# A transformer block's down projection in a seven-product form: 14 of 16 row pairs by seven block products instead of eight, two of the four weight sums made by adding transfers, and rows scaled by their norm before they are transposed

## The chip, the cores and the metric

One Trainium2 chip, one core of it. The time is the device time of one execution in microseconds. Three timed executions of the kernel before gave 305.18, 305.67 and 305.17 us (median 305.18); another execution was taken by the profiler and took 305.3 us, of which the span from the first to the last instruction is 303.2 us. TensorE (PE) multiplies matrices, VectorE (DVE) and ScalarE (ACT) work element by element, GpSimd (POOL) does a little of both kinds of odd work, and SyncE (SP) issues most transfers (DMAs).

## What is computed

One block on 256 rows of width 1024, all in float32: an attention mixer, a residual, and a squared-ReLU MLP with 4096 hidden columns, each between two RMS norms.

```python
h = x
u = rms_norm(h, norm_mix_pre)
u = moba_attention(u, w_qkv, w_o)          # 8 heads of 128; 256 rows are one block, so: causal, with slopes
h = h + rms_norm(u, norm_mix_post)
u = rms_norm(h, norm_ffn_pre)
u = square(relu(u @ w_up)) @ w_down        # w_up 1024 x 4096, w_down 4096 x 1024
h = h + rms_norm(u, norm_ffn_post)
```

## The kernel before

**Three matmuls for one product.** Every float32 operand is split into a high part (a copy rounded to the matmul's float32r type) and a low part (the rest). A product is three matmuls into one accumulator: high by high, high by low, low by high (`mm3`, lines 209 to 214). So each weight element passes ScalarE once (`whi`, line 83) and VectorE once (`wlo`, line 84), before TensorE can use it.

**The weights' pipeline.** The class `Weights` holds a list of 48 sources of 1 MB each: attention's, then the MLP's. `load` issues a source's transfer on SP into one of five raw buffers; `pump` splits the next quarter of a source (512 elements per partition: one instruction on ScalarE, one on VectorE) into one of four pairs of part buffers, and issues the next load when all four quarters of a source are split. `done` frees part buffers. The MLP's sources come as chunks of 512 hidden columns: `up0, up1, down0, up2, down1` and so on, `down7` last.

**The order of the work.** PE and SP run in the order in which the code is written. ScalarE and VectorE do so too in the stretches under `manual_schedule`; elsewhere a scheduler sets their order. PE runs through attention, then the out projection `o0`, `o1` (tiles `acc`), and then the MLP. The 256 rows are two tiles `t` of 128.

**From attention to the MLP** (lines 589 to 646). `PostNorm.take` squares and weighs a finished half row out of PSUM, `put` adds the residual into `xs`. The rows of tile 0 are transposed on PE (tile `ht`) from `xs`, in the middle of `o1`'s last 12 matmuls; `evac_x` takes them out of PSUM times the gain, as a high and a low part (`xT`). The transposed rows are not yet divided by their norm: this factor, `rstd2` (from `square_x` and `rstd_of`, whose power is taken on POOL), is applied later. For chunk 0, which has rows as PSUM's partitions (`up_first`, 512-column matmuls), it is a scalar per partition in the ReLU; for the other chunks, which have hidden columns as partitions, it is a row `rrow2` that `diag_of` and `row_of` make with four VectorE instructions and two matmuls.

**The MLP's loop** (lines 648 to 676). `up_chunk(c)`: 4 hidden blocks by 8 by 3 = 96 matmuls of 256 columns, and for each hidden block `up_evac` (ReLU and norm on VectorE, two squares on ScalarE, a difference on VectorE). `down_chunk(c - 1)`: 4 hidden blocks by 2 row tiles by 2 column halves by 3 = 48 matmuls of 512 columns into four accumulators `acd` that stay in PSUM to the end. Seen as pairs of hidden blocks, there are 16 pairs, and each pair takes 8 block products, 24 matmuls. The last chunk's down projection runs row tile by row tile (lines 682 to 690), with the last norm, the residual and the output's transfers behind each.

Of the kernel before, what the change touches and what calls it, by code (L numbers as in the profile page):

```python
# [8 lines left out]
F32 = mybir.dt.float32  # L9
# [12 lines left out]


# [4 lines left out]
class Weights:  # L28
# [4 lines left out]
    N = 2048  # L33

    def __init__(self, nc, raw_pool, part_pool, raw_bufs, part_bufs):
        self.nc, self.raw_pool, self.part_pool = nc, raw_pool, part_pool
        self.raw_bufs, self.part_bufs = raw_bufs, part_bufs
        self.sources, self.raw, self.parts, self.steps, self.split = [], {}, {}, [], set()
        self.loaded = self.finished = self.next = self.part = 0

    def add(self, src, how, cuts=1):
        self.sources.append((src, how, cuts))
        return len(self.sources) - 1

    def load(self, n=None):
# [17 lines left out]
    def slice(self, t, i, j):  # L63
        how = self.sources[i][1]
        if how == "cols":
            return t[:, :, j * P:(j + 1) * P]
        if how == "rows":
            return t[:, j // 2, (j % 2) * 512:(j % 2) * 512 + 512]
        return t[:, j, :]

    def pump(self, n, lo_engine=None):
        nc = self.nc
        while n > 0 and self.next < len(self.steps):
            i, j = self.steps[self.next]
            if i >= self.finished + self.part_bufs or i >= self.loaded:
                return
            if i not in self.parts:
                shape = list(self.raw[i].shape)
                self.parts[i] = [self.part_pool.tile(shape, F32R, name=f"w{p}{i}", tag=f"w{p}", bufs=self.part_bufs)
                                 for p in ("hi", "lo")]  # L80
            hi, lo = (self.slice(t, i, j) for t in self.parts[i])
            x = self.slice(self.raw[i], i, j)
            nc.scalar.activation(hi, x, AF.Copy)  # L83
            (lo_engine or nc.vector).tensor_tensor(lo, x, f32(hi), op=ALU.subtract)  # L84
            self.split.add((i, j))
            self.next += 1
            n -= 1
            if sum((i, q) in self.split for q in range(4)) == 4:
                self.load()

    def get(self, i, j):
        while (i, j) not in self.split:
# [3 lines left out]
        return self.parts[i]  # L96
# [6 lines left out]
def block(ctx: ExitStack, tc: tile.TileContext, x, g_mix_pre, g_mix_post, g_ffn_pre, g_ffn_post,  # L103
# [80 lines left out]

    ident = const.tile([P, P], F32, name="ident")
# [8 lines left out]
    dist = const.tile([P, 384], F32, name="dist")  # L194
# [12 lines left out]
    oT = [const.tile([P, HEADS, S], F32R, name=f"oT{i}") for i in range(2)]  # L207

    def mm3(ps, a, b, start, stop):


        nc.tensor.matmul(ps, lhsT=a[0], rhs=b[0], start=start, stop=False)  # L212
        nc.tensor.matmul(ps, lhsT=a[0], rhs=b[1], start=False, stop=False)  # L213
        nc.tensor.matmul(ps, lhsT=a[1], rhs=b[0], start=False, stop=stop)  # L214
# [38 lines left out]
    def transpose_x(k, t):  # L253
        o = (k // 4) * S + t * P
        nc.tensor.transpose(banks[k % 4][:, o:o + P], xs[:, t, k * P:(k + 1) * P], ident)

    def evac_x(k, g0, a=0, b=S):
        o = (k // 4) * S
        split_psum_scaled((xT[0][:, k, a:b], xT[1][:, k, a:b]), banks[k % 4][:, o + a:o + b],
                          gT[:, g0 + k:g0 + k + 1])  # L260
# [10 lines left out]

    qk_pool = tc.alloc_tile_pool(name="qk_pool", bufs=1)
# [443 lines left out]
```

## Time and profile before

| | |
|---|---|
| timed executions | 305.17, 305.18, 305.67 us |
| profiled execution, its span | 305.3 us, 303.2 us |
| granted TensorE clock, mean | 0.997 |
| PE busy | 294.5 us, 97% |
| weight loads on PE | 262.7 us, 87% |
| DVE busy | 194.5 us, 64% |
| ACT busy | 166.6 us, 55% |
| POOL busy | 18.5 us, 6% |
| read from HBM | 52.44 MB, 176 GB/s over the span |

A row of the timeline has the start, the duration, the engine, the line, the operation, and output<-inputs with their shapes; `[idle before <-releaser]` says how long the engine stood idle and what ended that. Rows of PE overlap: a matmul's row is longer than the step to the next one, and the step is what counts. In the groups by line, `x28 | 11.9, 424` is 28 instructions, 11.9 us in all, 424 ns each.

### The profile page before, as it was taken

Reading aid. Unit: us, or ns where it says so; the run is one execution under the profiler, and the core shown is the slowest. Engines: PE = TensorE matmul, PEld = TensorE weight load, DVE = VectorE, ACT = ScalarE, POOL = GpSimd, SP = SyncE. Lnnn points to the kernel's source line nnn. Section 1 sums busy time; section 2 is a strip of 40 time slices with the busy share of each in tenths; the row PEclk is TensorE's granted clock in tenths of the full one; section 3 lists DMA queues with packets and bytes.
Section 4 is the critical chain, followed back from the end, with each engine's and each line's share of the span. In section 5 each row is a group of like instructions: output and inputs, shape, how many; then the busy total and the mean of one; then the engine's idle time right before and its main releaser. Section 6 shows DMA issues by size and latency. Waiting matters only on the chain.

```text
span 303.2 us, 4863 instructions
## 1 busy us (share of the span) xinstructions
PE 294.5 (97%) x1838; PEld 262.7 (87%) x1838; DVE 194.5 (64%) x407; ACT 166.6 (55%) x395; POOL 18.5 (6%) x34
## 2 busy tenths in 40 slices
PE   7999999999999999999999999999999999999991
PEld 3889999988998888898898898898898898898880
DVE  2668989774689395999447547547547537537042
ACT  4767938665396265977526526526526526526020
POOL 4000133101200001000000000000000000000000
PEclk9999999999999999999999999999999999999998
DMA  6998595729404740087960960960950950300012
GB/s 189 367 394 308 200 391 176 268 99 378 148 2 145 272 118 22 0 291 262 332 228 9 344 205 11 334 211 11 347 197 16 338 203 10 130 0 3 0 45 93
DMA packets 22055, 53.79 MB, mean 177 GB/s; under 512 B 1024, under 2 KB 1808, under 8 KB 22032
## 3 DMA queue, kind: packets, MB, share of 16 engines
q1 hardware_dynamic: 21888, 53.16, 50.5%
q8 instruction: 14, 0.23, 0.3%
q10 hardware_dynamic: 144, 0.33, 0.3%
q14 instruction: 9, 0.07, 0.1%
HBM read 52.44 MB, written 1.05 MB: 176 GB/s over the span
## 4 chain that ended last, share of the span: by engine, by line
PE 93%; DVE 4%; DMA 1%; ACT 0%; issue 0%; DVEq 0%; ACTq 0%
PE psu L212 10%; PE psu L214 10%; PE psu L213 10%; PE acd L212 10%; PE acd L213 10%; PE acd L214 10%; PE psv L292 3%; PE psq L212 3%; PE psq L213 3%; PE psq L214 3%; PE psv L294 2%; PE acc L214 2%; PE acc L212 2%; PE psv L296 2%; PE acc L213 2%; DVE wlo L84 2%
## 5 line engine op out<-in xcount | busy, mean ns | idle before, releaser
L84 DVE TENSOR_TENSOR wlo<-raw,whi 128x512 fp32r<-128x512 f32 x186 | 121.0, 699 | 42.3 <-ACT whi L83 42.1
L83 ACT ACTIVATE whi<-raw 128x512 fp32r<-128x512 f32 x192 | 107.2, 623 | 47.6 <-PE acd L214 33.3
L212 PE MATMUL psu<-xT,whi 128*128 128x256 f32 x224 | 63.4, 283 | 0.0
L213 PE MATMUL psu<-xT,whi 128*128 128x256 f32 x224 | 63.3, 282 | 0.0
L214 PE MATMUL psu<-xT,wlo 128*128 128x256 f32 x224 | 62.9, 281 | 0.0
L213 PE MATMUL acd<-wlo,uhi 128*128 128x512 f32 x128 | 50.5, 395 | 0.0
L212 PE MATMUL acd<-whi,uhi 128*128 128x512 f32 x128 | 50.5, 395 | 0.0
L214 PE MATMUL acd<-whi,ulo 128*128 128x512 f32 x128 | 50.5, 394 | 0.0
L214 PEld LDWEIGHTS psu<-xT,wlo 128*128 128x128 f32 x224 | 42.5, 190 | 0.0
L213 PEld LDWEIGHTS psu<-xT,whi 128*128 128x128 f32 x224 | 42.1, 188 | 0.3
L212 PEld LDWEIGHTS psu<-xT,whi 128*128 128x128 f32 x224 | 42.0, 187 | 0.3
L556 ACT ACTIVATE uhi<-r 128x256 fp32r<-128x256 f32 x28 | 11.6, 413 | 35.0 <-DVE r L555 35.0
L214 PEld LDWEIGHTS acd<-whi,ulo 128*128 128x128 f32 x128 | 24.1, 188 | 5.6
L213 PEld LDWEIGHTS acd<-wlo,uhi 128*128 128x128 f32 x128 | 24.1, 188 | 5.3
L212 PEld LDWEIGHTS acd<-whi,uhi 128*128 128x128 f32 x128 | 24.1, 188 | 5.3
L558 DVE TENSOR_TENSOR ulo<-u,uhi 128x256 fp32r<-128x256 f32 x28 | 11.9, 424 | 14.4 <-ACT u L557 14.4
L555 DVE SCALAR_TENSOR_TENSOR r<-psu,rrow 128x256 f32<-128x256 f32 x28 | 11.8, 422 | 13.7 <-PE psu L214 13.7
L212 PE MATMUL psq<-xT,whi 128*128 128x256 f32 x64 | 18.4, 288 | 0.0
L212 PE MATMUL psk<-xT,whi 128*128 128x256 f32 x64 | 18.4, 287 | 0.0
L214 PE MATMUL psq<-xT,wlo 128*128 128x256 f32 x64 | 18.1, 282 | 0.0
L213 PE MATMUL psq<-xT,whi 128*128 128x256 f32 x64 | 18.1, 282 | 0.0
L214 PE MATMUL psk<-xT,wlo 128*128 128x256 f32 x64 | 18.0, 282 | 0.0
(121 smaller groups left out, 432.7 us busy)
## 6 DMA issues: line engine op xcount, KB each, us to landing
raw<-in_w_up_dram SPq DMA_DIRECT2D x16, 1024.0 KB, 6.1
raw<-in_w_down_dram SPq DMA_DIRECT2D x16, 1024.0 KB, 7.5
raw<-in_attn_w_qkv_dram SPq DMA_DIRECT2D x10, 1024.0 KB, 8.6
raw<-in_attn_w_o_dram SPq DMA_DIRECT2D x4, 1024.0 KB, 4.9
raw<-in_attn_w_qkv_dram SPq DMA_DIRECT2D x8, 256.0 KB, 6.2
xs<-in_x_dram SPq DMA_DIRECT2D x2, 256.0 KB, 6.0
xs<-in_x_dram SPq DMA_DIRECT2D x1, 512.0 KB, 7.1
g_mix<-in_norm_mix_post_dram SPq DMA_DIRECT2D x1, 512.0 KB, 7.2
```

The source lines that it names most:

```text
L83: nc.scalar.activation(hi, x, AF.Copy)
L84: (lo_engine or nc.vector).tensor_tensor(lo, x, f32(hi), op=ALU.subtract)
L212: nc.tensor.matmul(ps, lhsT=a[0], rhs=b[0], start=start, stop=False)
L213: nc.tensor.matmul(ps, lhsT=a[0], rhs=b[1], start=False, stop=False)
L214: nc.tensor.matmul(ps, lhsT=a[1], rhs=b[0], start=False, stop=stop)
L292: nc.tensor.matmul(psv[0][t], lhsT=x0[t], rhs=w[0], start=first, stop=False)
L294: nc.tensor.matmul(psv[0][t], lhsT=x1[t], rhs=w[0], start=False, stop=False)
L296: nc.tensor.matmul(psv[0][t], lhsT=x0[t], rhs=w[1], start=False, stop=last)
L555: nc.vector.scalar_tensor_tensor(r, ps[:, :S], 0.0, rrow2, op0=ALU.max, op1=ALU.mult)
L556: nc.scalar.activation(hi, r, AF.Square)
L558: nc.vector.tensor_tensor(lo, u, f32(hi), op=ALU.subtract)
```

## The change

**Seven products for a pair.** For a pair `q` of hidden blocks (two blocks of 128 hidden columns), the hidden values form a 2 by 2 grid of blocks (two row tiles, two hidden blocks), and so does the down weight (two hidden blocks, two column halves of 512). The seven-product form (Winograd's variant of Strassen's) replaces the 8 block products by 7, on 4 sums of hidden blocks and 4 sums of weight blocks. The sums of the results are linear, so each of the seven products accumulates over 14 pairs in a PSUM bank of its own (`M1` to `M7`), and they are combined once, after pair 13. Pairs 14 and 15 are added in the plain form onto the combined accumulators.

**Where the sums are made.** Hidden sums: three VectorE instructions per pair (`combine`). Weight sums: two of the four are made by transfers: SP loads one block of the weights twice side by side (`sums`, tag `sum`), and later POOL issues a transfer that adds two other blocks onto them (`accum_op=add`). The other two sums are two VectorE additions (`add_up`). A pair's down weights are now two units of split work: `blocks` (3 blocks, 1536 elements per partition) and `sums` (4 blocks, 2048).

**Larger split instructions, a fixed order.** In the MLP a whole unit is split by one instruction on ScalarE (`W.hi`) and one on VectorE (`W.lo`); ScalarE, VectorE and POOL follow the written order to the end. The up projection goes pair by pair (`up_pair`, 48 matmuls of 256 columns, with 1 KB per partition row of its load), one PSUM bank for both hidden blocks; the down projection of pair `q - 2` follows it.

**Rows divided by their norm first.** `scale_h` takes `rstd2` and writes the scaled rows into `yg` before they are transposed, so that `rrow2`, `diag_of` and `row_of` go for the MLP. The hidden values then need only a ReLU and a square, both on ScalarE.

The core of the diff:

```diff
+    def load(self, n=None):
...
+        if i in self.sevens:
+            self.raw[i] = self.raw_pool.tile([P, 3, 512], F32, name=f"raw{i}", tag="raw", bufs=self.raw_bufs)
+            self.nc.sync.dma_start(self.raw[i][:, 0:1, :], src[:, 0:1, 0:512])
+            self.nc.sync.dma_start(self.raw[i][:, 1:3, :], src[:, 1, :].rearrange("p (h c) -> p h c", c=512))
...
+    def sum_by_loads(self):
+        nc = self.nc
+        for i in self.to_add:
...
+            nc.gpsimd.dma_start(self.sums[i][:, 0:2, :], both, accum_op=ALU.add)
+        self.to_add = []
+        while self.begun < min(len(self.sevens), self.summed + self.SUM_BUFS):
...
+            nc.sync.dma_start(self.sums[i][:, 0:2, :], self.sources[i][0][:, 0:1, 512:1024].broadcast_to([P, 2, 512]))
+            self.to_add.append(i)
+    def add_up(self, u):
...
+        self.nc.vector.tensor_tensor(t[:, 2, :], raw[:, 2, :], t[:, 0, :], op=ALU.add)
+        self.nc.vector.tensor_tensor(t[:, 3, :], raw[:, 1, :], t[:, 2, :], op=ALU.add)
+    def hi(self, u, h=None):
...
+        self.nc.scalar.activation(self.half(self.parts[u][0], h), self.half(x, h), AF.Copy)
+    def lo(self, u, h=None):
...
+        self.nc.vector.tensor_tensor(lo, x, f32(hi), op=ALU.subtract)
...
+        if kind == "sums":
+            self.summed += 1
+            self.sum_by_loads()
+        else:
+            self.load()
...
+    PRODUCTS = (("M1", A11, 0, 0), ("M2", A12, 0, 1), ("M3", S4, 0, 2), ("M5", S1, 1, 0),
+                ("M7", S3, 1, 1), ("M6", S2, 1, 2), ("M4", A22, 1, 3))
...
+    def combine(q):
+        x = hidden[q]
+        tt = nc.vector.tensor_tensor
+        tt(x[:, S3:S1 + 1, :], x[:, A11:A22 + 1, :], x[:, A21:A21 + 1, :].broadcast_to([P, 2, P]), op=ALU.subtract)
+        tt(x[:, S2, :], x[:, S1, :], x[:, A11, :], op=ALU.add)
+        tt(x[:, S4, :], x[:, A12, :], x[:, S2, :], op=ALU.subtract)
...
+        def scale_h(t):
+            rstd_of(ssq2[:, 0, t:t + 1], ssq2[:, 1, t:t + 1], rstd2[:, t:t + 1])
+            for c in range(2):
+                s = slice(c * 512, (c + 1) * 512)
+                nc.vector.tensor_scalar(yg[:, t, s], xs[:, t, s], rstd2[:, t:t + 1], None, op0=ALU.mult)
...
         for c in range(2):
             norms[0].put(xs, c * 512, (c + 1) * 512)
+            square_x(0, ssq2, (c,))
+        scale_h(0)
         last_rows("o1", act_o, 1, 0)
         norms[1].take(0)
-        last_rows("o1", act_o, 1, 1, turn_first)
+        last_rows("o1", act_o, 1, 1)
...
+        W.sum_by_loads()
+        for k in range(KT):
+            transpose_x(k, 0, yg)
+        evac_x(0, KT, 0, P)
+        evac_x(1, KT, 0, P)
         norms[1].take(1)
+        for k in range(2, 5):
+            evac_x(k, KT, 0, P)
...
+        scale_h(1)
+        W.sum_by_loads()
...
         for k in range(KT):
             up_first(0, k)
-            if k == 4:
-                turn(0, 1, 2, 3)
+        for k in range(KT):
+            transpose_x(k, 1, yg)
...
+    def down_pair(q, products):
+        hi, lo = act[q]
+        for name, slot, e, j in products:
...
+            mm3(M[name], a, w, q == 0, q == NP - 3)
+        W.done(1)
...
+        for q in range(4, NP):
+            d = q - LAG
+            if q + 1 < NP:
+                W.hi(piece[f"up{q + 1}"])
+                combine(q - 1)
+            hidden_hi(q - 1)
+            if q + 1 < NP:
+                W.lo(piece[f"up{q + 1}"])
+            hidden_lo(q - 1)
+            below = piece[f"down{d + 1}"]
+            if d + 2 < NP - 1:
+                W.add_up(below + 1)
+            ps = up_pair(q)
...
+            up_relu(q, ps)
+            if q + 1 < NP:
+                W.hi(below)
+            W.lo(below)
...
+            down_pair(d, PRODUCTS[:3])
+            W.hi(below + 1)
+            up_square(q)
+            W.lo(below + 1)
+            down_pair(d, PRODUCTS[3:])
...
+        nc.scalar.activation(m1, M["M1"], AF.Copy)
+        tt(u2, m1, M["M6"], op=ALU.subtract)
+        tt(M["M2"], M["M2"], m1, op=ALU.add)
+        tt(u3, M["M7"], u2, op=ALU.add)
+        tt(u4, M["M5"], u2, op=ALU.add)
+        nc.vector.scalar_tensor_tensor(M["M5"], M["M5"], -1.0, u3, op0=ALU.mult, op1=ALU.subtract)
+        tt(M["M4"], M["M4"], u3, op=ALU.add)
+        tt(M["M3"], M["M3"], u4, op=ALU.subtract)
```

**What moves on PE.** At the end of `o1`, before: the eight transposes of tile 0 (`ht`) stand between the last 12 matmuls of `acc` (row 682 comes after the same four tiles a second time).

```order
673 L214 MATMUL acc_1_1195<-whi_1208,oT_124 128x512
674 L255 MATMUL ht_1354<-ident,xs 128x128
675 L255 MATMUL ht_1355<-ident,xs 128x128
676 L255 MATMUL ht_1356<-ident,xs 128x128
677 L255 MATMUL ht_1357<-ident,xs 128x128
682 L212 MATMUL acc_1_1195<-whi_1208,oT_123 128x512
```

In the changed kernel they stand behind all of `acc`, directly ahead of the first matmul of `up_first` (`psu_0`), and read the scaled rows `yg` (again the four tiles come twice).

```order
682 L301 MATMUL acc_1_1198<-whi_1299,oT_130 128x512
683 L343 MATMUL ht_1356<-ident,yg 128x128
684 L343 MATMUL ht_1357<-ident,yg 128x128
685 L343 MATMUL ht_1358<-ident,yg 128x128
686 L343 MATMUL ht_1359<-ident,yg 128x128
691 L299 MATMUL psu_0_1522<-whi_1366,xT_127 128x512
```

The same is done with tile 1: its transposes stood inside `up_first`, and now stand between `up_first(0, ...)` and `up_first(1, ...)`.

**What moves on VectorE there.** Before, at the same place: the residual of tile 0 (`xs`), the first half of tile 1's norm (`mss`, `yg`), and at once the low parts of the transposed rows.

```order
168 L533 SCALAR_TENSOR_TENSOR xs<-yg,rs,xs 128x512 x2
169 L527 TENSOR_SCALAR mss<-ss 128x1
170 L530 TENSOR_TENSOR yg<-acc_0_1194,g_mix 128x512
171 L222 SCALAR_TENSOR_TENSOR xT_122<-ht_1354,gT,xT_121 128x128
172 L222 SCALAR_TENSOR_TENSOR xT_122<-ht_1355,gT,xT_121 128x128
```

In the changed kernel the mean square (`ms`) and the scaling (`yg<-xs,rstd`) come in between, and the second half of tile 1's norm stands between the low parts.

```order
168 L623 SCALAR_TENSOR_TENSOR xs<-yg,rs,xs 128x512 x2
169 L318 SCALAR_TENSOR_TENSOR ms<-ssq_1352 128x1
170 L719 TENSOR_SCALAR yg<-xs,rstd_1353 128x512 x2
171 L617 TENSOR_SCALAR mss<-ss 128x1
172 L620 TENSOR_TENSOR yg<-acc_0_1197,g_mix 128x512
173 L352 SCALAR_TENSOR_TENSOR xT_128<-ht_1356,gT,xT_127 128x128
174 L352 SCALAR_TENSOR_TENSOR xT_128<-ht_1357,gT,xT_127 128x128
175 L617 TENSOR_SCALAR mss<-ss,mss 128x1
```

**VectorE in the MLP's loop.** In the changed kernel one pair's work reads as follows: the hidden sums (`x`), the low parts of the next up weights and of the hidden blocks (`ulo`), the two weight sums, and the low parts of the pair's `blocks` and `sums`.

```order
249 L655 TENSOR_TENSOR x_2150<-x_2150 128x256
250 L656 TENSOR_TENSOR x_2150<-x_2150 128x128
251 L657 TENSOR_TENSOR x_2150<-x_2150 128x128
252 L134 TENSOR_TENSOR wlo_2169<-raw_1972,whi_2168 128x2048
253 L671 TENSOR_TENSOR ulo_2175<-x_2150,uhi_2174 128x896
254 L114 TENSOR_TENSOR sum_1948<-raw_2032,sum_1948 128x512
255 L115 TENSOR_TENSOR sum_1948<-raw_2032,sum_1948 128x512
256 L134 TENSOR_TENSOR wlo_2235<-raw_2032,whi_2234 128x1536
257 L134 TENSOR_TENSOR wlo_2251<-sum_1948,whi_2250 128x2048
```

Before, a pair had eight quarters `wlo` of 512 elements (two units) and two rows each of `r` and `ulo` (256 elements). All that stands ahead of `o1`'s norms is in the same order in both kernels on PE, VectorE and ScalarE.

More of the change, by code (lines that the diff above doesn't have):

```diff
@@ L28 @@
 class Weights:
-    N = 2048
+    STEPS = {"cols": 4, "k": 4, "rows": 4, "whole": 1, "blocks": 1, "sums": 1}
+    SUM_BUFS = 3
     def __init__(self, nc, raw_pool, part_pool, raw_bufs, part_bufs):
@@ new lines, in add_up, with half @@
+    def add_up(self, u):
+        i, _ = self.units[u]
+        raw, t = self.raw[i], self.sums[i]
+        self.nc.vector.tensor_tensor(t[:, 2, :], raw[:, 2, :], t[:, 0, :], op=ALU.add)
+        self.nc.vector.tensor_tensor(t[:, 3, :], raw[:, 1, :], t[:, 2, :], op=ALU.add)
+    def half(self, t, h):
+        return t if h is None else t[:, h * t.shape[1] // 2:(h + 1) * t.shape[1] // 2, :]
+    def hi(self, u, h=None):
+        i, kind = self.units[u]
+        assert u < self.finished + self.part_bufs and i < self.loaded, (u, self.finished, i, self.loaded)
+        x = self.sums[i] if kind == "sums" else self.raw[i]
+        if u not in self.parts:
+            self.parts[u] = [self.part_pool.tile(list(x.shape), F32R, name=f"w{p}{u}", tag=f"w{p}", bufs=self.part_bufs)
+                             for p in ("hi", "lo")]
+        self.nc.scalar.activation(self.half(self.parts[u][0], h), self.half(x, h), AF.Copy)
@@ L71, in pump @@
+    def lo(self, u, h=None):
+        i, kind = self.units[u]
+        x = self.sums[i] if kind == "sums" else self.raw[i]
+        hi, lo, x = (self.half(t, h) for t in (*self.parts[u], x))
+        self.nc.vector.tensor_tensor(lo, x, f32(hi), op=ALU.subtract)
+        if h == 0:
+            return
+        if kind == "sums":
[3 more added lines that the diff above has]
+            self.load()
     def pump(self, n, lo_engine=None):
@@ L95, in get @@
             assert self.next > n
-        return self.parts[i]
+        return self.parts[u]
     def done(self, n):
@@ L662, in down_chunk @@
-    def down_chunk(c):
-        for f in range(4):
-            for t in range(NT):
-                for n in range(2):
-                    a = [b[:, f, t * P:(t + 1) * P] for b in up[c]]
-                    rows_unit(f"down{c}", f, a, t, n, c == 0 and f == 0, False)
-            if f % 2:
-                W.done(1)
-            W.pump(2)
-    for c in range(1, NC):
-        up_chunk(c)
-        if c == 1:
-            acc = [[bank(mm, f"acd{t}_{n}") for n in range(2)] for t in range(NT)]
-        down_chunk(c - 1)
+                w = [a[:, k, f * P:(f + 1) * P] for a in W.parts[piece[f"up{q}"]]]
@@ L677, in block, with plain @@
+    def plain(q, t, c, f, end=False):
+        a = [b[:, 2 * f + t, :] for b in act[q]]
+        w = [b[:, f, c * 512:(c + 1) * 512] for b in W.parts[piece[f"down{q}"]]]
+        mm3(acc[t][c], a, w, False, end, True)
+    for t, c in ((1, 0), (0, 1), (0, 0), (1, 1)):
+        for f in range(2):
+            plain(NP - 2, t, c, f)
+    W.done(1)
+    ctx.enter_context(tc.manual_schedule(engines=ELEMENTWISE))
     ov = out[0].rearrange("(t p) d -> p t d", p=P)
-    def act_down(f, t):
-        return [b[:, f, t * P:(t + 1) * P] for b in up[NC - 1]]
@@ L684, in block @@
         for c in range(2):
-            last_rows(f"down{NC - 1}", act_down, t, c)
+            for f in range(2):
+                plain(NP - 1, t, c, f, f == 1)
             norm.take(c)
@@ L689, in block @@
             queue.dma_start(ov[:, t, a:b], yg[:, t, a:b])
-    W.done(2)
+    W.done(1)
 _INS = ["x", "norm_mix_pre", "norm_mix_post", "norm_ffn_pre", "norm_ffn_post", "w_up", "w_down",
```

285 lines of the change are left out of this document (189 added, 96 removed).

## The prediction

> **What bounds the kernel now.** I read the page's busy times first, then the chain that ended last, then TensorE's waits, then the timeline of single stretches. The first line below is part 1 of the page, the second the shares of the chain by engine, the last two TensorE's waits by total.
>
> ```profile
> PE 294.5 (97%) x1838; PEld 262.7 (87%) x1838; DVE 194.5 (64%) x407; ACT 166.6 (55%) x395; POOL 18.5 (6%) x34
> PE 93%; DVE 4%; DMA 1%; ACT 0%; issue 0%; DVEq 0%; ACTq 0%
> PE psidle L412 <- DVE idle L415: 1.2, 1, 1.2
> PE xt L255 <- DMA xs<-in_x_dram: 1.0, 1, 1.0
> ```
>
> TensorE is the bound from end to end: it waits twice, 2.2 us in all, both at the start. So a matmul less is worth its step, and a new wait costs its length. The steps come from the timeline of PE: the first row is the MLP's first 256-column matmul after chunk 0, then come the first and the one-past-last of a `down_chunk` (48 matmuls), of an `up_chunk` (96), and the last matmul.
>
> ```profile
> 126.37 0.28 PE L212 MATMUL psu<-xT,whi 128*128 128x256 f32 x1
> ...
> 160.97 0.40 PE L212 MATMUL acd<-whi,uhi 128*128 128x512 f32 x1
> ...
> 172.12 0.28 PE L212 MATMUL psu<-xT,whi 128*128 128x256 f32 x1
> ...
> 183.65 0.40 PE L212 MATMUL acd<-whi,uhi 128*128 128x512 f32 x1
> ...
> 296.42 0.40 PE L214 MATMUL acd<-whi,ulo 128*128 128x512 f32 x1
> ```
>
> A 512-column matmul steps by 11.15/48 = 0.232 us, a 256-column one by 11.53/96 = 0.120 us. Check: 672 x 0.120 + 384 x 0.232 + 0.44 for four transposes = 170.2 us, and from 126.37 to 296.65 are 170.3. Nothing else is in there.
>
> **Products saved.** 14 pairs by 1 product by 3 matmuls = 42 matmuls by 0.232 = **-9.75 us**, if TensorE never waits in the loop. A pair then takes 48 x 0.120 + 21 x 0.232 = 10.64 us instead of 11.34. The feeding engines must manage a pair in that time.
>
> **VectorE's work per pair.** No row shows 2048 or 1536 elements at once. The rows that show how its time grows, and ScalarE's beside them (mean ns after the comma):
>
> ```profile
> L84 DVE TENSOR_TENSOR wlo<-raw,whi 128x512 fp32r<-128x512 f32 x186 | 121.0, 699 | 42.3 <-ACT whi L83 42.1
> L558 DVE TENSOR_TENSOR ulo<-u,uhi 128x256 fp32r<-128x256 f32 x28 | 11.9, 424 | 14.4 <-ACT u L557 14.4
> L333 DVE TENSOR_TENSOR q<-psq,q 128x128 fp32r<-128x128 f32 x8 | 2.3, 287 | 0.5 <-ACT q L332 0.3
> L556 ACT ACTIVATE uhi<-r 128x256 fp32r<-128x256 f32 x28 | 11.6, 413 | 35.0 <-DVE r L555 35.0
> L83 ACT ACTIVATE whi<-raw 128x512 fp32r<-128x512 f32 x192 | 107.2, 623 | 47.6 <-PE acd L214 33.3 <-DMA raw<-in_attn_w_qkv_dram 5.8 <-issue 4.7
> ```
>
> From 128 to 512 the time is 0.15 us plus 1.075 ns per element. By that line 2048 elements take 2.35 us, 1536 take 1.80, 896 take 1.11; about 0.06 less where the next instruction doesn't depend on it. A pair: low parts of up and of `sums` 2 x 2.29, of `blocks` 1.74, of the hidden blocks 1.05, two weight sums 1.43, three hidden sums 1.09 (each needs the one before) = **9.9 us of 10.64**. From above, 8064 elements at the row's whole 699 per 512 give 11.0 us. I take 9.9: three rows lie on one line with a fixed part, and larger instructions pay that part once. ScalarE by its own line (0.20 + 0.82 ns per element): 5632 elements of `whi`, 896 hidden, 512 ReLU, 512 square = 7.1 us.
>
> **Does the loop's order let TensorE run?** With the pair's up projection from 0 to 5.76 and down from there to 10.64: ScalarE splits the next up weights from 0.1 (their buffer is freed by the last down matmul), VectorE works from 1.6 on: hidden sums to 2.7, up low parts to 5.0, hidden low parts to 6.0, weight sums to 7.5. `blocks` can be split only after the up projection and its ReLU: ScalarE 6.7 to 8.1, VectorE to 9.9; `sums` to 9.95 and 12.2, which is 1.6 of the next pair. The up weights are ready 5.6 us before TensorE wants them. At the start there is less room: from the up projection of pair 2 on VectorE has 20.6 us of work up to pair 4's low parts (2.55 until the first hidden tile is squared, 16.9 of work by the prices above, 1.2 waiting for pair 3's ReLU), and TensorE comes for them after 2 x 5.76 + 0.44 + 2 x 4.88 = 21.7. So 1.1 us are spare there, and about 0.7 more with each pair. Cost taken: nothing; if VectorE were 5% slower (10.4 a pair), still nothing; at 10% (10.9) about 0.6 us there and 0.25 with each pair after it, 3 to 4 us.
>
> **From attention to the MLP** is where TensorE will wait. Rows of this stretch, from the timelines of PE, ScalarE, VectorE and POOL:
>
> ```profile
> 109.38 1.41 DVE L533 SCALAR_TENSOR_TENSOR xs<-yg,rs,xs 128x512 f32<-128x512 f32 x2
> 110.64 1.03 PE L255 MATMUL ht<-ident,xs 128*128 128x128 f32 x8
> 111.43 0.47 PE L212 MATMUL acc<-whi,oT 128*128 128x512 f32 x1
> 111.39 2.17 ACT L221 ACTIVATE xT<-ht,gT 128x128 fp32r<-128x128 f32 x8 [0.50 <-PE ht L255]
> 113.62 0.40 PE L212 MATMUL psu<-whi,xT 128*128 128x512 f32 x1
> 114.49 0.68 ACT L226 ACTIVATE sq<-xs 128x512 bf16<-128x512 f32 x1
> 115.30 0.63 ACT L226 ACTIVATE sq<-xs 128x512 bf16<-128x512 f32 x1
> 115.84 0.19 ACT L226 ACTIVATION_READ_ACCUMULATOR sq<-xs 128x1 f32 x1
> 123.22 0.16 DVE L231 SCALAR_TENSOR_TENSOR ms<-ssq 128x1 f32<-128x1 f32 x1 [0.36 <-ACT sq L226]
> 123.46 0.55 POOL L232 TENSOR_TENSOR rstd<-ms,power 128x1 f32<-128x1 f32 x1 [3.79 <-DVE ms L231]
> 124.04 0.29 DVE L239 TENSOR_SCALAR diag<-ident,rstd 128x128 fp32r<-128x128 f32 x1
> L366 DVE TENSOR_SCALAR s<-s,st 128x256 f32<-128x256 f32 x8 | 2.8, 348 | 0.1
> L572 DVE TENSOR_SCALAR r<-psu,rstd 128x512 f32<-128x512 f32 x2 | 1.5, 748 | 0.0
> ```
>
> Tile 0: the residual is there at 110.8 as before; its squares run from 110.2, 0.81 apart, with the last sum read at 111.7; mean square, power and the way back to VectorE take 0.82 (123.22 to 124.04): 112.6. One scaling instruction lies between 0.35 (256 elements, from SBUF) and 0.75 (512, from PSUM); I take 0.48, nearer the SBUF row: 0.35, plus 256 elements more at the growth from the diagonal's row (0.29 for 128) to it. Both are done at 113.5. ScalarE starts 0.75 after the first transpose (110.64 to 111.39), its first part takes 0.37, so `up_first` starts at 114.5; before, at 113.62. TensorE itself comes free at 113.62 - 0.79 = 112.8. Tile 1: half of its norm now queues behind the first two `evac_x` on ScalarE and VectorE, its residual behind three more low parts (117.6), so the squares end at 119.4, the scaled rows at 121.1; TensorE has finished `up_first(0)` at 120.2 and starts the second one at 122.2. With 24 steps and four transposes that ends at 128.2, where before 126.37: **+1.9**, I put **+2.0**. Bounds: +0.9 if transposes follow the scaling half by half, +3.2 with 0.75 per scaling. The 0.23 us of `row_of` that go are in this difference.
>
> **The end.** The combination (8 VectorE instructions by about 0.6 to 0.75) follows the order M1, M2, M6, M7, M5, M4, M3, and its first sum, on M2, is ready 1.3 us before TensorE wants it; the 24 matmuls of pair 14 hide the rest, and the low parts of pair 15's weights come 1.2 us early. Behind the last matmul now:
>
> ```profile
> 296.92 0.60 ACT L226 ACTIVATE scr<-acd 128x512 bf16<-128x512 f32 x1 [2.10 <-PE acd L214]
> 297.63 0.21 DVE L527 TENSOR_SCALAR mss<-ss,mss 128x1 f32<-128x1 f32 x1 [2.03 <-ACT scr L226]
> 298.55 1.41 DVE L533 SCALAR_TENSOR_TENSOR yg<-yg,rs,xs 128x640 f32<-128x640 f32 x2
> ```
>
> A row tile's part is now 12 matmuls (2.8 us) and not 24, so tile 0's residual and norm still occupy VectorE when tile 1's halves come. The last residual starts about 2.3 us behind the last matmul instead of 1.9: **+0.4**, between 0 and 1.
>
> **Transfers.** Per pair: up 1 MB, blocks 0.75, first load of `sums` 0.5, adding transfer 0.5. The third row is a one-off load of 512 KB, with its time to landing:
>
> ```profile
> 7.50:20.00 12.50, 12.50 (x61) 10.18 (x60) 7.80 (x14) 9.10 (x23) 0.00 (x0) 1.00 1.03 378
> 161.00:183.60 22.60, 22.60 (x146) 20.49 (x145) 12.99 (x25) 11.39 (x25) 0.00 (x0) 1.00 0.55 187
> g_mix<-in_norm_mix_post_dram SPq DMA_DIRECT2D x1, 512.0 KB, 7.2
> ```
>
> At the 378 GB/s of the first row the plain 2.25 MB take 6.0 us. No adding transfer is in this trace: as a plain one it takes 1.3 us, as slow as the third row 7.2. I take 2.7, since it also reads what it adds to; then 8.7 of 10.64 us are used (in the loop of before the share is 0.55), and each adding transfer has some 15 us from issue to use. Cost: nothing.
>
> **Sum:** 305.3 - 9.75 + 2.0 + 0.4 = 297.95; the profiled execution lies 0.1 over the median of the timed ones, so **297.8 us**. Its own range: transition and end at their bounds and up to 1 us of waits at pair 4 give 296.5 to 300.
>
> **Rivals.**
>
> *VectorE becomes the bound.* The trace shows how POOL could do it:
>
> ```profile
> 35.44 1.30 POOL L84 TENSOR_TENSOR wlo<-raw,whi 128x512 fp32r<-128x512 f32 x1 [12.63 <-ACT whi L83]
> 35.50 1.79 DVE L84 TENSOR_TENSOR wlo<-raw,whi 128x512 fp32r<-128x512 f32 x1
> ```
>
> Beside POOL's instruction VectorE's took 1.79 instead of 0.69. If issuing an adding transfer held it so once a pair, a pair would cost 11.0 us, and 14 x 0.36 = 5 us come back: about 303. Against it: these are two operations that read the same kind of operands, and issuing a transfer isn't. The Trainium skill ("SBUF — State Buffer", Who interferes with whom) says that a VectorE instruction with two SBUF inputs contends with a GpSimd instruction that reads SBUF, not with one that only writes it. The row agrees with the first half; by the second half the issue, which writes descriptors, would cost nothing. Chance 0.12.
>
> *TensorE's clock falls in the new gaps.* The window behind the last matmul:
>
> ```profile
> 297.00:303.00 6.00, 0.00 (x0) 0.00 (x0) 2.22 (x4) 0.60 (x2) 0.55 (x1) 0.88 0.23 87
> ```
>
> Its granted clock is 0.88, the loop's is 1.00. The change makes two stretches without matmuls, 112.8 to 114.5 and 120.2 to 122.2. Were each followed by a stretch as long at half speed, half of 1.7 + 2.0 is lost, 1.9 us: 299.9. The Trainium skill ("TensorE: Matmul & The Clock Gate", Part 1) has the clock halved after an idle window of about 3.4 us, and the warm-up just as long. By that rule neither gap is long enough; if one were, 1.7 us would go each time, an estimate from that page. Chance 0.07.
>
> *Transfers become the bound, and the kernel gets slower.* In the loop the adding transfers decide: from 10.64 - 6.0 = 4.6 us for 0.5 MB on, TensorE waits; from 5.2 on, a pair costs 11.16 and the gain is gone. At 7.2 us a pair costs 13.2: 298 + 14 x 2.6 = 334. For it: nothing like it is in the trace; against it: 7.2 is a landing time beside other loads, and five raw buffers stay two pairs ahead. Chance 0.09.
>
> That the change doesn't do what it says is out: PE's written order has 1764 rows instead of 1808.
>
> **Chances.** As forecast 0.72, VectorE 0.12, clock 0.07, transfers 0.09. The range 296.5 to 301.6 holds the first nearly whole, the clock's, and a mild form of VectorE's, about 0.8. What differs by less than 0.2% (0.6 us) can't be told from no change here. Faster: the first three but for VectorE's worst, 0.89; same 0.02; slower 0.09.
>
> **What would show it.** Right: TensorE's waits are two new groups, on `ht` and `xT`, of ahead of `ht` and ahead of `psu`, of together about 2.1 us (0.9 and 1.2); pairs step by 10.64; VectorE 90 to 95% busy in the loop. Wrong: waits of PE on `wlo` or `ulo` (VectorE), of VectorE on `sum` from POOL's queue (transfers), a granted clock under 0.95 between 113 and 127, or a scaling instruction far from 0.48.

## The result, and the profile after

The changed kernel took **297.66 us** (median of 4 runs, 296.42 to 298.43) against 305.19 for the kernel before: ratio 0.9746, 95% interval 0.9706 to 0.9785. The forecast was 297.8. The profiled execution took 296.42 us, its span is 294.6.

Busy times and shares of the chain of the page after:

```profile
PE 285.7 (97%) x1794; PEld 253.5 (86%) x1794; DVE 238.9 (81%) x366; ACT 189.5 (64%) x311; POOL 35.5 (12%) x48
PE 87%; DVE 5%; issue 2%; DMA 2%; ACT 2%; POOL 1%; SPq 1%; DVEq 0%; POOLq 0%
```

TensorE is still busy for 97% of a span that is 8.6 us shorter; VectorE went from 64% to 81%. The groups of waits of PE and of the weight loads (PEld) that are new between attention and MLP (columns: total us, times, longest; PE and PEld can show the same stop):

```profile
PE ht L343 <- DVE yg L719: 0.5, 2, 0.3
PEld ht L343 <- DVE yg L719: 1.0, 2, 0.8
PEld psu L299 <- ACT xT L350: 0.7, 2, 0.4
PEld psu L301 <- DVE xT L352: 0.7, 3, 0.3
PEld ht L343 <- PE acc L301: 0.6, 1, 0.6
```

No wait on `wlo` or `ulo` is in the list. The timeline of PE after, at the marks by which the kernels are compared: the first key matmul, the last of the output projection, each tile's transposes and the matmul behind them, pair 2's first 256-column matmul, two pairs of the loop, the last matmul:

```profile
31.02 0.28 PE L299 MATMUL psk<-xT,whi 128*128 128x256 f32 x1
...
111.47 0.40 PE L301 MATMUL acc<-whi,oT 128*128 128x512 f32 x1
112.08 1.06 PE L343 MATMUL ht<-ident,yg 128*128 128x128 f32 x8 [0.20 <-DVE yg L719]
113.27 0.50 PE L299 MATMUL psu<-whi,xT 128*128 128x512 f32 x1
...
118.81 0.40 PE L301 MATMUL psu<-whi,xT 128*128 128x512 f32 x1
119.53 1.34 PE L343 MATMUL ht<-ident,yg 128*128 128x128 f32 x8 [0.32 <-DVE yg L719]
121.00 0.50 PE L299 MATMUL psu<-whi,xT 128*128 128x512 f32 x1
...
127.28 0.28 PE L299 MATMUL psu<-xT,whi 128*128 128x256 f32 x1
...
148.99 0.28 PE L299 MATMUL psu<-xT,whi 128*128 128x256 f32 x1
...
159.63 0.28 PE L299 MATMUL psu<-xT,whi 128*128 128x256 f32 x1
...
287.67 0.39 PE L301 MATMUL acM<-whi,ulo 128*128 128x512 f32 x1
```

Before, the first key matmul starts here:

```profile
32.09 0.28 PE L212 MATMUL psk<-xT,whi 128*128 128x256 f32 x1
```

The same marks, subtracted, show where the time went (us):

| stretch | before | after | difference |
|---|---|---|---|
| start to first key matmul | 32.09 | 31.02 | -1.07 |
| key matmul to pair 2 (attention, transition) | 94.28 | 96.26 | +1.98 |
| pair 2 to last matmul (the loop) | 170.05 | 160.39 | -9.66 |
| last matmul to end | 6.78 | 6.93 | +0.15 |
| span | 303.2 | 294.6 | -8.6 |

The change doesn't touch the first row; the experiments return to it. A pair steps by 159.63 - 148.99 = 10.64. The next rows are windows: the two stretches with the new gaps, then a part of the loop (busy us of PE, PEld, DVE, ACT, POOL, then granted clock, DMA share, GB/s):

```profile
113.00:120.00 7.00, 6.55 (x30) 4.70 (x28) 5.47 (x15) 5.94 (x16) 2.12 (x4) 1.00 0.90 295
120.00:127.30 7.30, 7.14 (x35) 5.38 (x34) 6.76 (x13) 6.48 (x14) 2.83 (x3) 1.00 0.96 161
...
159.63:244.81 85.18, 85.18 (x554) 77.80 (x553) 77.69 (x74) 60.26 (x50) 10.70 (x9) 1.00 1.01 287
```

The third row holds eight pairs: TensorE has no gap, VectorE is busy 77.69/8 = 9.71 us a pair (91%), ScalarE 7.5 (forecast 7.1), and the clock is 1.00 in all three.

### The profile page after: what moved, and what is told of

Its sections match the earlier page's. It is cut to its first block, busy times and chain, and to the rows that moved or that the text cites. A ratio compares the mean times of both kernels' runs of the same rounds, so it can differ in the third digit from the quotient of the medians.

```text
span 294.6 us, 4748 instructions
## 1 busy us (share of the span) xinstructions
PE 285.7 (97%) x1794; PEld 253.5 (86%) x1794; DVE 238.9 (81%) x366; ACT 189.5 (64%) x311; POOL 35.5 (12%) x48
## 3 DMA queue, kind: packets, MB, share of 16 engines
q1 hardware_dynamic: 33088, 56.83, 56.6%
q0 software_dynamic: 3808, 7.34, 14.3%
## 4 chain that ended last, share of the span: by engine, by line
PE 87%; DVE 5%; issue 2%; DMA 2%; ACT 2%; POOL 1%; SPq 1%; DVEq 0%; POOLq 0%
PE psu L299 10%; PE psu L301 10%; PE psu L300 10%; PE acM L300 9%; PE acM L299 9%; PE acM L301 9%; PE psq L299 3%; PE psq L300 3%; PE psq L301 3%; DVE wlo L155 3%; PE psv L384 2%; PE psv L382 2%; PE psv L386 2%; PE acc L301 2%; PE acc L300 2%; PE acc L299 2%
## 5 line engine op out<-in xcount | busy, mean ns | idle before, releaser
L134 DVE TENSOR_TENSOR wlo<-raw,whi 128x1536 fp32r<-128x1536 f32 (+2 forms) x32 | 61.3, 1920 | 6.3 <-ACT whi L128 6.2
L155 DVE TENSOR_TENSOR wlo<-raw,whi 128x512 fp32r<-128x512 f32 x66 | 45.1, 719 | 12.7 <-ACT whi L154 12.6
L128 ACT ACTIVATE whi<-raw 128x1536 fp32r<-128x1536 f32 (+2 forms) x32 | 51.7, 1616 | 2.2 <-PE acM L301 2.1
L154 ACT ACTIVATE whi<-raw 128x512 fp32r<-128x512 f32 x72 | 41.3, 628 | 12.8 <-DMA raw<-in_attn_w_qkv_dram 5.2
L300 PE MATMUL acM<-wlo,uhi 128*128 128x512 f32 x114 | 45.1, 396 | 0.0
L299 PE MATMUL acM<-whi,uhi 128*128 128x512 f32 x114 | 45.0, 395 | 0.0
L301 PE MATMUL acM<-whi,ulo 128*128 128x512 f32 x114 | 44.9, 394 | 0.0
L134 DVE TENSOR_TENSOR wlo<-sum,whi 128x2048 fp32r<-128x2048 f32 x14 | 32.1, 2293 | 5.3 <-ACT whi L128 5.3
L128 ACT ACTIVATE whi<-sum 128x2048 fp32r<-128x2048 f32 x14 | 26.9, 1920 | 7.9 <-issue 2.9
L301 PEld LDWEIGHTS acM<-whi,ulo 128*128 128x128 f32 x114 | 21.5, 189 | 5.0
```

Of the source, the lines that this page charges most:

```text
L128: self.nc.scalar.activation(self.half(self.parts[u][0], h), self.half(x, h), AF.Copy)
L134: self.nc.vector.tensor_tensor(lo, x, f32(hi), op=ALU.subtract)
```

## The experiments

My theory: TensorE stays the bound, 42 matmuls fewer are worth their steps, and the transition gives 2 us back; VectorE and the transfers are close behind. The rivals were VectorE, the clock and the transfers. Ratios are to the kernel before, with 95% intervals.

**The same kernel again.** No edit.

> The changed kernel once more, unchanged. Its four times lay between 296.4 and 298.4 us, those of the kernel before within 0.5. In the profiled run of 296.42 us the first matmul of the V projection started at 5.80, in the kernel before at 6.60, with the wait for the first part of x (1.0 us) gone. If the spread comes from when the first loads land, this profile shows a start later than 5.80 by about what its time is above 296.4, and the span between the first query matmul and the last matmul is 268.7 us as in the first profile, within 0.3. If it comes from the loop or the transition, the start is the same and that span is longer.

297.74 us (296.81 to 298.67), 0.975 (0.9722 to 0.9778). The first key matmul came at 31.41 instead of 31.02, all later marks 0.39 to 0.40 later, and pair 2 to the last matmul took 160.39 us again. So the spread comes from the start. In the kernels below, which share this part, the first key matmul lies between 31.5 and 33.2. The kernel before spreads as well: 304.32 to 306.66 in 17 runs. The -1.07 of the table is luck of one execution. The other three rows of the table add up to -7.53, and that is also the difference of the medians, 297.66 and 305.19.

**One product more, one fewer, two fewer.**

```diff
             mm3(M[name], a, w, q == 0, q == NP - 3)
+            if name == "M4" and 0 < q < NP - 3:
+                mm3(M[name], a, w, False, False)
```

> An eighth product (three 512-column matmuls of operands already there, onto the bank of M4, which makes the result meaningless) in 12 of the 14 pairs: 36 matmuls. Theory, TensorE is the bound and the other engines have room: +36 x 0.2325 = +8.4 us, 306.0, a pair at 11.34. Rival, the loop is partly held by VectorE or the adding transfers although no wait shows: clearly less, +4 to +7.

306.27 us, 1.0017 (0.9995 to 1.0038). A pair steps 11.33, pair 2 to the last matmul takes 168.55 us: +8.16. With the eighth product back in 12 pairs nothing is left of the gain.

```diff
         for name, slot, e, j in products:
+            if name == "M6" and 0 < q < NP - 3:
+                continue
```

> The product M6 left out in 12 of the 14 pairs (36 matmuls; the result is meaningless). TensorE then needs 9.95 us a pair. VectorE is busy 9.71 of 10.64 in the trace. If its two idle stretches of a pair (0.29 and 0.78, both behind ScalarE's whi) can shrink, the pair goes to about 9.95 and the time to 297.7 - 8.4 = 289.3, with no wait in the loop. If they can't (ReLU, whi and the low parts follow the up projection in one chain), VectorE keeps 10.3 to 10.64 a pair, waits of TensorE on wlo or ulo appear, and only 0 to 4 us are gained. Forecast: 289 to 292.

288.99 us, 0.9462 (0.9432 to 0.9493): 8.75 less than the 297.74 of the change. A pair steps 9.93, the loop takes 151.79 us, and TensorE waits for nothing in it. So VectorE's idle stretches do shrink. And with M7 left out too:

```diff
+            if name in ("M6", "M7") and 0 < q < NP - 3:
+                continue
```

> Two products, M6 and M7, left out in 12 of the 14 pairs (meaningless result). TensorE needs 9.25 us a pair, VectorE is busy 9.71. Theory, VectorE is next to the bound: a pair goes to 9.8 to 9.9 (the step of VectorE's weight sums where it catches up is 9.86), TensorE waits on wlo or ulo, and the time is 287 to 288, only 1 to 2 us under the kernel with one product left out (289.0). Rival, VectorE follows TensorE's pace with room to spare: 289.0 - 8.4 = 280.6.

288.20 us, 0.9442 (0.9413 to 0.9471): only 0.8 less, where VectorE's side of the expectation had 1 to 2 and the other 8.4. A pair steps 9.85, and these groups of waits appear in the kernel with five products:

```profile
PE psu L301 <- DVE wlo L134: 1.7, 10, 0.2
PEld psu L301 <- DVE wlo L134: 3.9, 11, 0.4
PEld psu L299 <- ACT r L677: 3.6, 10, 0.4
```

VectorE's bound, its short waits for ScalarE included, is 9.85 us a pair; the change uses 10.64 and so stands 0.8 us from it. The transfers are the same as in the change, and in this loop VectorE waits for none of them.

**The weight sums without adding transfers.** The lines that issue them go, and VectorE adds:

```diff
-            nc.gpsimd.dma_start(self.sums[i][:, 0:2, :], both, accum_op=ALU.add)
...
+        self.nc.vector.tensor_tensor(t[:, 0:2, :], t[:, 0:2, :], raw[:, 0:3:2, :], op=ALU.add)
         self.nc.vector.tensor_tensor(t[:, 2, :], raw[:, 2, :], t[:, 0, :], op=ALU.add)
```

> No adding transfers: VectorE itself adds blocks to the two loaded copies, one instruction of 1024 elements more for each of the 14 pairs (1.2 us), as the weight sums it already makes; the transfers fall by 0.5 MB a pair. Theory, VectorE is next to the bound: busy 9.71 + 1.2 = 10.9 of 10.64 us, so the loop goes by VectorE's pace (seen as 9.86 a pair where it runs unheld, so 11.06) and 12 to 13 pairs lose 0.3 to 0.45: 301.5 to 304, with waits of TensorE on wlo or ulo. Rival, VectorE's idle time was real room, or the adding transfers themselves slowed it: 298 or less.

304.72 us, 0.9984 (0.9964 to 1.0004): the whole gain of the change is gone. The first two steps behind pair 4 are 10.64 and 10.91, while VectorE still has a lead; the later ones are 11.10 to 11.13 (once 11.40), so 0.47 more than in the change. The expectation had 0.3 to 0.45 and 301.5 to 304, so the loss came out larger. From pair 2 to the last matmul it took 167.68 us, 7.29 more; 2.5 of that fall behind the start of pair 15 (24.10 us instead of 21.57), where VectorE's combination is no longer hidden:

```profile
PE acM L295 <- DVE acM L876: 0.8, 1, 0.8
...
PEld acM L296 <- DVE wlo L130: 3.8, 11, 1.0
PEld psu L297 <- DVE wlo L130: 3.3, 10, 0.3
```

The new instruction takes 1.22 us; 9.86 + 1.22 = 11.08, near the 11.11 of most pairs. So the adding transfers are what pays for the seven-product form here.

**Each adding transfer twice.**

```diff
             nc.gpsimd.dma_start(self.sums[i][:, 0:2, :], both, accum_op=ALU.add)
+            nc.gpsimd.dma_start(self.sums[i][:, 0:2, :], both, accum_op=ALU.add)
```

> Each adding transfer issued twice (the weight sums then hold a block twice, the result is meaningless): 0.5 MB more a pair. In the trace the 14 adding transfers took 14.3% of 16 queues over 294.6 us, 3.0 us each, and the plain 2.25 MB about 6.0 to 6.9 a pair. Theory, the transfers had 0.7 to 1.7 us of room in a pair: with 3.0 more they need 12.0 to 12.9 of 10.64, and after the lead of some pairs is used up TensorE waits: 10 to 12 pairs lose 1.4 to 2.3: 308 to 322. Rival, the adding transfers share the queues' idle time and have much room (the forecast's 2.7 from a price of 1.3): under 300.

328.12 us, 1.0726 (1.0672 to 1.078). Here the transfers are the bound: VectorE waits for an adding transfer in nearly every pair (12 times, 37.8 us in all). Two such waits of its timeline, twelve pairs apart:

```profile
144.36 0.69 DVE L115 TENSOR_TENSOR sum<-raw,sum 128x512 f32<-128x512 f32 x1 [2.85 <-DMA sum<-in_w_down_dram]
...
295.38 0.69 DVE L115 TENSOR_TENSOR sum<-raw,sum 128x512 f32<-128x512 f32 x1 [1.32 <-DMA sum<-in_w_down_dram]
```

So a pair takes 12.6 us on average; single ones take between 9.8 and 17.8, and three of TensorE's stops were followed by a lower clock (more below), which is in these times too. The queues' rows (packets, MB, share of 16 engines), two of the change and then one of this kernel, give the time of the transfers' packets:

```profile
q1 hardware_dynamic: 33088, 56.83, 56.6%
q0 software_dynamic: 3808, 7.34, 14.3%
```

```profile
q0 software_dynamic: 7616, 14.68, 25.8%
```

14.3% of 294.6 us by 14 are 3.0 us, 25.8% of 323.7 by 28 are 2.98. That is the price of one adding transfer. The plain loads take 166.7 us for 56.83 MB, so 6.9 for the 2.36 MB of a pair (2.25 times 1024 KB). By these prices a pair with two adding transfers needs 12.8, near the 12.6 on average, and one with a single adding transfer 9.9 of 10.64. This is an estimate. What is measured is the kernel with five products: it stepped 9.85 with these transfers and without a wait for them, so there are at least 0.8 us of room. Whether the time of the packets or the way of a sum from its load to the add, through three buffers, sets the pace of the doubled kernel, no run tells apart.

**The scaling left out.** The transposes read `xs`, and the instruction that makes `yg` from it goes:

```diff
-                nc.vector.tensor_scalar(yg[:, t, s], xs[:, t, s], rstd2[:, t:t + 1], None, op0=ALU.mult)
...
-            transpose_x(k, 0, yg)
+            transpose_x(k, 0)
```

> The scaling of the rows left out: the norm is still computed but the transposes read xs, so that TensorE need not wait for mean square, power and scaling (the hidden values are not normalised, which changes the result only). Theory, the transition costs 1.9 us in waits: the first 256-column matmul of pair 2, counted from the first query matmul of the same run, comes 1.9 us earlier (106.4 instead of 108.35), and the time is 295.8. Rival, the waits have another cause (low parts and evacuations queued on VectorE and ScalarE): it comes by less than 1 us earlier, and the time stays above 296.7.

296.29 us, 0.9706 (0.9677 to 0.9735). From the first key matmul to pair 2 it took 94.93 us instead of 96.26: 1.33 less, not 1.9. So neither side of the expectation was right. The other 0.65 of the loss stays, and the timeline of this kernel shows it:

```profile
112.82 1.03 PE L343 MATMUL ht<-ident,xs 128*128 128x128 f32 x8
113.98 0.50 PE L299 MATMUL psu<-whi,xT 128*128 128x512 f32 x1
```

The eight transposes take 0.8 of these 1.16 us. For the other 0.36, once for each tile, TensorE waits until the first part of `xT` has been evacuated, because nothing else stands between transposes and matmuls. In the kernel before, the matmuls of another block did.

**No scaling, and the transposes back among the matmuls.** The row's factor cancels in the norm behind the MLP but for epsilon, so nothing need wait for it:

```diff
-        last_rows("o1", act_o, 1, 1)
+        last_rows("o1", act_o, 1, 1, lambda: turn(0, *range(KT)))
...
+            if k == 4:
+                turn(1, 0, 1, 2, 3)
...
+                nc.vector.scalar_tensor_tensor(eps2, ms2, EPS, ms2, op0=ALU.mult, op1=ALU.mult)
```

> The rows are not scaled at all; the norm behind the MLP divides the row's factor out again, and its epsilon is multiplied by the square of the row's mean square (two instructions of two elements), so the result is the reference's. The transposes read xs and stand among the matmuls as in the kernel before (tile 0 inside the last rows of the output projection, tile 1 inside up_first), and the squares move into pairs 6 to 9, into ScalarE's idle time ahead of the ReLU. Theory, all of the transition's loss goes: from the first query matmul to pair 2's first 256-column matmul 106.15 us (106.38 of before less 0.23 for row_of) instead of 108.35 and of 107.03 with the scaling alone left out: 297.7 - 2.2 = 295.5. Rival, the loop starts with VectorE or ScalarE further behind and waits at pair 4, or the squares delay the ReLU: the stretch is won but the loop gives back 0.5 to 2: 296 to 298.

293.54 us, 0.9624 (0.9598 to 0.9649): faster than both kernels, and by 2 us more than expected. From the first key matmul to pair 2 it took 93.67 us, 2.59 less than the change; but the loop, whose matmuls are the same, took 158.95 instead of 160.39. That is the next question.

**32 bytes of padding.**

```diff
+    pad = const.tile([P, 8], F32, name="pad")
```

> The changed kernel with 32 bytes per partition reserved behind the constants and nothing else, so that every tile behind them (raw weights, whi, wlo, yg, the hidden values) starts 32 bytes later; whi and wlo then start at 32 modulo 64 as xT does, where they started at 0. The kernel without scaling had these addresses by chance (a new constant of two columns), its 256-column matmuls took 280 ns in the mean where those of all others took 283, its pair stepped 10.54 instead of 10.65, and it was 1.5 us faster in the loop and 0.6 in the attention than its edits explain. If the place of the weights is the cause: 10.54 a pair here too, 1.4 us less from pair 2 to the last matmul (159.0 instead of 160.39), 0.6 less from the first key matmul to the last of the output projection, 295.7. If the cause is in that kernel's other edits: 10.65 and 297.7.

295.76 us, 0.9692 (0.9664 to 0.9719), as the first side of the expectation, the place of the tiles, has it. The groups of PE by line, the change and then this kernel (last numbers: busy us and mean ns of one):

```profile
L299 PE MATMUL psu<-xT,whi 128*128 128x256 f32 x224 | 63.4, 283 | 0.0
...
L299 PE MATMUL acM<-whi,uhi 128*128 128x512 f32 x114 | 45.0, 395 | 0.0
```

```profile
L299 PE MATMUL psu<-xT,whi 128*128 128x256 f32 x224 | 62.7, 280 | 0.0
...
L299 PE MATMUL acM<-whi,uhi 128*128 128x512 f32 x114 | 45.0, 395 | 0.0
```

The pair steps 10.54, the loop takes 158.95 us, and from the first key matmul to pair 2 pass 95.89 (0.37 less; up to the last matmul of the output projection it is 0.40, where the expectation had 0.6). The kernel with the transposes back among the matmuls has its weights at the same place as this one. Taking 0.37 from the 2.59 above leaves 2.22 for the transition, the 2.2 that was expected. With xT moved as well:

```diff
+    padx = const.tile([P, 8], F32, name="padx")
     xT = [const.tile([P, KT, S], F32R, name=f"xT{i}") for i in range(2)]
```

> The same with 32 bytes ahead of xT and 32 behind it: xT, whi and wlo all start at 0 modulo 64. If what counts is that weights and moving operand start alike modulo 64, the pair steps 10.54 and the time is 295.7; if the weights must lie at 32 modulo 64, or xT alone counts, 10.65 or more and 297.7.

295.14 us, 0.9672 (0.9645 to 0.9698), the loop 158.96: it isn't the place of the weights modulo 64 alone.

**The first adding transfers held until the scaling is done.**

```diff
         scale_h(1)
+        held = small.tile([P, 1], F32, name="held")
+        nc.gpsimd.tensor_copy(held, yg[:, 1, D - 1:D])
         W.sum_by_loads()
```

> Ahead of the first three adding transfers POOL copies one element per partition of the last scaled row, so that it issues them only after the scaling of tile 1 and no longer beside it (118.98 for 3.85 us in the trace, where that scaling took 1.17 us against 0.88 for tile 0). The rival that POOL's issue slows VectorE: tile 1's scaling takes 0.88, and pair 2's first 256-column matmul comes 0.2 to 0.3 us earlier against the last matmul of the output projection (15.5 to 15.6 us behind it instead of 15.81). If the issue does nothing: 1.17 stays, and 15.81. In the time at most 0.3 us, 297.4 to 297.7.

The scaling of both tiles on VectorE, in the change and then here:

```profile
111.44 0.88 DVE L719 TENSOR_SCALAR yg<-xs,rstd 128x512 f32<-128x512 f32 x2 [0.66 <-POOL rstd L319]
...
118.98 1.17 DVE L719 TENSOR_SCALAR yg<-xs,rstd 128x512 f32<-128x512 f32 x2 [0.66 <-POOL rstd L319]
```

```profile
112.93 0.88 DVE L719 TENSOR_SCALAR yg<-xs,rstd 128x512 f32<-128x512 f32 x2 [0.66 <-POOL rstd L319]
120.47 0.88 DVE L719 TENSOR_SCALAR yg<-xs,rstd 128x512 f32<-128x512 f32 x2 [0.66 <-POOL rstd L319]
```

The last matmul of the output projection stood at 112.96, pair 2 began at 128.48: 15.52 us, 0.29 less than in the change. The issue does slow this scaling. The kernel without adding transfers, which has nothing to issue there, shows the same: the scaling of tile 1 took 0.88, and pair 2 began 15.51 us behind the last matmul of the output projection. The time of the kernel with the late issue, 296.10 (0.97, 0.9674 to 0.9726), says more than that by accident: the new small tile moved `uhi` and `ulo` by 128 bytes, their 512-column matmuls took 389 to 391 ns instead of 395, and the loop 158.93.

**All operands at one place.** The kernel with no scaling and the transposes back, with reserved bytes that put both kinds of operand at 224 modulo 256.

```diff
+    padc = const.tile([P, 16], F32, name="padc")
+    pads = small.tile([P, 1], F32, name="pads")
```

> The kernel without scaling, with reserved bytes that put xT, whi, wlo, uhi and ulo at the same place modulo 256 (224). In the runs so far 256-column matmuls took 280 ns in the mean where xT and whi lay 0 or 64 apart modulo 256, 283 where 96; 512-column ones of the down projection 390 where whi and ulo lay 0 apart, 395 where 128. Theory, the distance of the two operands counts: both gains come together here, 280 (or less, if 0 is better than 64) and 390, a pair steps 10.54 - 0.10 = 10.44, pair 2 to the last matmul takes 157.5 us instead of 158.95, and the time is 293.5 - 1.5 = 292.0. Rival, the 390 of the late issue had another cause (the late start of the adding transfers): 395, 10.54 and 293.5.

293.07 us (292.23 to 293.55), 0.9609 (0.958 to 0.9637): not to be told from 293.54. The 512-column matmuls took 389 to 390, the 256-column ones 283 again. So the first half of the expectation held, and "the nearer the better" fell. The loop took 158.62.

## Why the prediction was right

The number was right, and so was the mechanism: the three terms of the sum measure -9.66, +1.98 and +0.15, where the forecast had -9.75, +2.0 and +0.4. One term was off by 0.25 us, and the plain transfers, which were put at no cost, were priced too low. One thing was luck: the steps were taken over from the kernel before, and they held because the operands' places modulo 256 are the same in both kernels (means of 283 and 395 ns in both). With 32 bytes of padding the same change measured 295.76, below the forecast's range of 296.5 to 301.6.

- **Products saved.** Forecast -9.75 at 10.64 a pair; measured -9.66 at 10.64. One product more and one fewer in 12 pairs (36 matmuls by 0.2325 are 8.37) moved the loop by +8.16 and -8.60, so TensorE's steps set it on both sides.
- **VectorE.** Forecast 9.9 a pair, upper bound 11.0; measured 9.71 busy, and 9.86 where it runs unheld. Its instructions lie on the line of the prediction: 2.28 to 2.29 for 2048 elements (2.35), 1.75 for 1536 (1.80), 1.08 for 896 (1.11). ScalarE's 7.1 was added up too low: its own line gives 7.4 for its six instructions, and 7.5 was measured. Rows of VectorE after:

```profile
145.06 2.28 DVE L134 TENSOR_TENSOR wlo<-raw,whi 128x2048 fp32r<-128x2048 f32 x1
...
148.27 0.68 DVE L114 TENSOR_TENSOR sum<-raw,sum 128x512 f32<-128x512 f32 x1
...
197.59 0.69 DVE L114 TENSOR_TENSOR sum<-raw,sum 128x512 f32<-128x512 f32 x1
```

  The last two lie five pairs apart: 49.32/5 = 9.86, so VectorE began behind and caught up by 0.78 us a pair. The first row is pair 4's low part: it ends at 147.34, TensorE comes for it at 148.99. The slack was 1.65, forecast 1.1.
- **The transition.** Forecast +2.0 with waits of 0.9 and 1.2; measured +1.98. Tile 0: TensorE is free at 111.70, its transposes start at 112.08 and take 0.8, the first matmul comes at 113.27: 0.77. Tile 1: 119.04, 119.53, 121.00: 1.16. The scaling took 0.44 for 0.48 at tile 0, 0.59 at tile 1; mean square, power and the way back 0.82 as taken. What the prediction didn't separate is that a third of the loss, 0.65, is the place of the transposes and not the norm.
- **The end.** Forecast +0.4, measured +0.15. The step that failed is "tile 0's residual and norm still occupy VectorE when tile 1's halves come". The rows of the end:

```profile
286.96 1.42 DVE L623 SCALAR_TENSOR_TENSOR yg<-yg,rs,xs 128x640 f32<-128x640 f32 x2
288.30 0.15 DVE L617 TENSOR_SCALAR mss<-ss 128x1 f32<-128x1 f32 x1
288.36 0.68 DVE L620 TENSOR_TENSOR yg<-acM,g_ffn 128x512 f32<-128x512 f32 x1
288.96 0.20 DVE L617 TENSOR_SCALAR mss<-ss,mss 128x1 f32<-128x1 f32 x1
289.08 0.68 DVE L620 TENSOR_TENSOR yg<-acM,g_ffn 128x512 f32<-128x512 f32 x1
289.86 1.42 DVE L623 SCALAR_TENSOR_TENSOR yg<-yg,rs,xs 128x640 f32<-128x640 f32 x2
```

  Tile 0's residual does run until 288.3, behind the last matmul. But ScalarE has read the last sum of squares only at 288.83:

```profile
288.64 0.19 ACT L313 ACTIVATION_READ_ACCUMULATOR scr<-acM 128x1 f32 x1
```

  The row that takes it starts at 288.96, 1.29 after that matmul began (1.21 before). So VectorE's other work is through by then but for about 0.1 us.
- **Transfers.** Forecast 2.7 us for an adding transfer and 8.7 a pair; by the queues' rows 3.0 and 9.9. What was sized wrong is the plain loads: 6.0 took the best rate of a short window and 2.25 million bytes where there are 2.36 (6.2 at that rate); the queue's row has 6.9. That the transfers cost nothing held, as the missing waits show, with less room than the forecast gave. The rival was near: a second one a pair makes the kernel 7.3% slower than before.
- **VectorE held by POOL.** Half wrong as a mechanism. In the loop nothing is held: beside the issue at 209.64 a low part of 1536 elements took 1.76, elsewhere 1.75 to 1.76. The scaling was held, 0.29 us once. The Trainium skill ("SBUF — State Buffer", Who interferes with whom) lists `tensor_scalar` among the instructions that can enter a two-port mode, which contends with GpSimd. The rows agree: 1.17 beside the issue, 0.88 without, in the kernel with the late issue and in the one without adding transfers. The prediction had cited only the rule for two SBUF inputs.
- **The clock.** 1.00 in both stretches with gaps, so the rival fell. How near it was, the kernel with doubled adding transfers shows on PE:

```profile
145.05 0.39 PE L300 MATMUL acM<-whi,uhi 128*128 128x512 f32 x1
147.50 0.50 PE L301 MATMUL acM<-wlo,uhi 128*128 128x512 f32 x1 [2.06 <-DVE wlo L135]
...
148.85 0.63 PE L300 MATMUL acM<-whi,uhi 128*128 128x512 f32 x1
...
151.83 0.52 PE L301 MATMUL acM<-wlo,uhi 128*128 128x512 f32 x1
```

  After a stop of 2.2 us the matmuls from 148.85 to 151.83 stepped 0.43 instead of 0.23, which lost 1.4 us. Its stops of 3.4 and 5.3 us were followed by the same, its stops of up to 1.0 us were not. The Trainium skill ("TensorE: Matmul & The Clock Gate", Part 1) speaks of an idle window of about 3.4 us; here 2.2 were enough, once, so the page is no safe margin. The change's own gaps, at most 1.2 us with transposes inside, did not do it.

## What to carry to other kernels

When TensorE is the bound, price a removed matmul at its step, then ask which engine or queue must absorb the work that replaces it, and how far that is from its own bound: here VectorE stood 0.8 us a pair away, and without the adding transfers the whole gain was gone. Waits at a change of phase are priced by the chain to the first matmul behind it, evacuation included, and transposes are best placed where other matmuls cover it. A scale that a later norm divides out need not be waited for.

## What the runs showed of the hardware that was not expected

- **The place of operands in SBUF changes a matmul's step.** 32 bytes of padding took 1.44 us off the loop (256-column matmuls 283 to 280 ns), 128 bytes ahead of `uhi` 1.46 (512-column ones 395 to 390). Distance of the two operands modulo 256 and mean ns: for 256 columns 64 apart 280, 96 apart 283, 0 apart 283; for 512 columns 128 apart 395, 0 apart 390. A rule that fits both isn't settled; the place of one operand alone could also explain them.
- **The DMA share is no measure of room.** It read 1.01 in the loop after (0.55 before), and yet the kernel with five products had the same transfers done in 9.85 us a pair instead of 10.64.
- **Two microseconds of spread lie in the first 30 us.** The first key matmul lay between 31.0 and 33.2 in the fourteen profiled executions, of the kernel before, the change and its variants. The six that have the stretch from there to pair 2 unchanged took 96.26 to 96.27 us for it.
